# A two-layer trunk: new load and matmul orders in the first stage, fewer edge operations, deeper weight prefetch and a rearranged tail in the last output stage

## Chip, cores and metric

One core of one Trainium2 chip. The metric is the device time of one execution in microseconds (us), as a median of several runs. The engines are TensorE (PE), VectorE (DVE), ScalarE (ACT), GpSimd (POOL) and SyncE (SP), which here issues the transfers between HBM and on-chip memory (SBUF); TensorE's results land in PSUM banks.

## What is computed

One denoising step of a hybrid trunk with two layers, on 128 context tokens and 1024 latent tokens of width 1024 (inner width 2048). Latent tokens get a position embedding over a grid that is 64 wide. Cut to what matters:

```python
def _layer(x, cond, p, kind, h0):
    shift, scale, gate = _ada(cond, w_ada, b_ada)          # silu(cond) @ w_ada + b_ada
    h = _rmsnorm(x, norm_g) * (1.0 + scale) + shift
    u, z = jnp.split(h @ w_in, 2, axis=-1)
    if kind == 0:
        y = _fourier_mix(u, p["w_fmix"], p["b_fmix"])      # real 2-D FFT by group, then a matmul
    else:
        ...                                                # convolution, two RG-LRU scans
    out = (y * jax.nn.silu(z)) @ w_out
    return x + gate * out, state

def _fourier_mix(u, w_fmix, b_fmix):
    ug = u.astype(jnp.float32).reshape(B, S, N_FGROUPS, FG_DIM)
    f = jnp.real(jnp.fft.fft2(ug, axes=(1, 3), norm="ortho"))
    y = jnp.einsum("bsgi,gij->bsgj", f, w_fmix).reshape(B, S, D_INNER)
    return y + b_fmix
```

Layer 0 is of kind 0, layer 1 of kind 1. Behind layer 1 stands one more RMSNorm with the weight `final_g`.

## The kernel before, in words

Every matmul of size is done in three (`mm3`, L238 to L240): operands are split into a high half in a rounded format and the low rest (`split`, L227 and L228, or `split_ops`, L433 and L437: the high half is a cast on ACT, the low half a subtraction on DVE, for some on POOL), and TensorE multiplies high by high, low by high and high by low. Tile names end in `h` and `l` accordingly.

**First stage (0 to about 109 us).** The Fourier transform over tokens is done as matmuls with DFT tables, before the projection: nine tiles of 128 tokens (`x0` the context, `x1` to `x8` the latents) are loaded, get their position embedding, are normalised (`norm`, L468 to L494), and are added and subtracted in pairs (`halves`, `d` L502 and `x` L505). Meanwhile the mixer's weights `w_fmix` are folded with a small DFT (`fold`; `Ah`, `Al`, `Bh`, `Bl` are its results), and the conditioning rows are made from `w_adaN` (`ada_part`; row copy `hot`, L578; columns `adc`). Results are scaled by the conditioning into `Qo` (odd frequencies) and `Qr` (even ones and the context; `put`, L616 on ACT, L620 on DVE). The columns of frequency zero and of the Nyquist frequency are replaced at the end by values collected in `k0r` (L747 to L764, then L769 and L770 for each of the eight blocks `c` of `Qr`).

This stage is written as a `Plan`: each operation is added with a planned cost and its reads and writes, a list scheduler then fixes the order on each engine, and operations given with two costs may go to DVE or POOL. Three strings set what is not left to it: `DORD` is the order of SP's loads (`x` tiles, `w` weights of the mixer, `t` DFT tables, `s` and `h` conditioning weights, `p` positions, `c` the small DFT, `a` a table for x0, `q` a table for the context, `L` the first projection weights), `PORD` and `RORD` are the order of the blocks on TensorE (`f` fold, `j` tables and pair n, `t` and `u` token matmuls, `s` and `h` conditioning, `o` and `q` results, `F` the last token matmuls `psF`, `U` the first half of the projection).

The position embedding is loaded as one 80x512 table; for each 128-token tile of the grid, DVE marks a one-hot matrix (`mark`, L413), TensorE spreads the table by it (`spread`, L417), and ACT copies four of six results to SBUF (`keep`, L427). Adds of it to x are L468 and L471.

**Mixer (to about 256 us).** A loop over eight groups `g`: `uweights(g + 1)` loads two weight tiles `uL`, `uR` and forms their sum and difference (L856, L857) and splits them; `umat(g)` multiplies them with `Qo` and `Qr` (accumulators `pu`, splits `uh` L888 and `ul` L889); `ymat(g - 1)` applies the folded weights (`pa`, `p`, `qb`, `y`). At `g == 0` stands the `prologue` (L802): the Nyquist row `nyq`, and `rb`, the inverse norms of all tokens spread over the partitions (nine scalings `dg` of the identity, L828, matmuls L829, copies to SBUF). POOL streams the normalised input of the z projection through `norm_stream` (L839): load `nt`, add positions (L792), multiply by `rb` (L844), apply the conditioning (L846), store to `hD`; three of 24 pieces in each group. Behind the loop, `h_load` reads them back (`hr`, `hh`, `hl`), and the last `ymat` stands behind the first of these in program order.

**z stage, output stage of layer 0, layer 1, output stage of layer 1 (256 to 1483 us).** Outside the Plan, the framework's own scheduler orders the instructions; program order, dependencies and the number of buffers of each pool decide what may go early. `out_stage` (L1043) multiplies three column chunks `c` of 384 tokens with eight tiles `m` of `w_out`, each in two half tiles that are loaded two half tiles ahead; on each result DVE adds the residual (L1107), ACT squares it (L1113), DVE sums the squares into `ssum` (L1114). In layer 1, `norm_steps` turns the sum into an inverse norm: matmuls with ones (`r`, L1054), small operations, `dg` (L1059), a matmul that spreads it (`b`, L1067); then DVE multiplies the eight results by it and by `final_g` (L1455), and SP stores each to `yT`.

Of the kernel before, what the change touches and what calls it, by code (L numbers as in the profile page):

```python
# [32 lines left out]
PORD = 'j0 f0 t40 f1 j1 f2 u42 t41 f3 s0 u52 j2 s1 t62 j3 t63 s2 s3 o0 h0 u74 u64 o3 o6 o4 o7 h1 q0 o1 q1 o2 o5'  # L33
RORD = 'h2 F2 F0 F4 h3 F5 F3 F1 F7 U0 F6 U1'
# [153 lines left out]
def body(tc, nc, a):  # L188
# [147 lines left out]
    P = Plan({"raw": 3, "hi": 4, "lo": 4, "xs": 4, "d": 2, "dr": 2, "dh": 4, "ps": 8}, fixed=("SP", "PE"), handles={"DVE": V, "POOL": PL})  # L336
# [63 lines left out]


    hot = xp.tile([128, 512], F32, name="hot")
    posR, posC = [None] * 4, [None] * 2
    for n, (kind, i) in enumerate((("R", 0), ("C", 0), ("R", 2), ("C", 1), ("R", 1), ("R", 3))):
        oh = hot[:, i * 128:i * 128 + 128]
        lo, hi = (0, 64) if kind == "C" else (64, 80)

        def mark(kind=kind, i=i, oh=oh, lo=lo, hi=hi):
            if kind == "C":
                e = ident[lo:hi, 32 * i:32 * i + 32].rearrange("p (o c) -> p o c", o=1).broadcast_to([64, 4, 32])  # L410
            else:
                e = ident[lo:hi, 64 + 4 * i:68 + 4 * i].rearrange("p (r o) -> p r o", o=1).broadcast_to([16, 4, 32])
            V.tensor_copy(oh[lo:hi].rearrange("p (r c) -> p r c", r=4), e)  # L413

        def spread(n=n, kind=kind, i=i, oh=oh, lo=lo, hi=hi):
            T["ps", f"p{n}"] = ps(f"pos{kind}{i}")
            PE.matmul(T["ps", f"p{n}"], oh[lo:hi], T["dr", "pos"][lo:hi], start=True, stop=True)  # L417
        xa(P.add("DVE", 0.22, mark, w=[("hot", n)]))
        xa(P.add("PE", 1.9, spread, r=[("hot", n), ("dr", "pos")], w=[("ps", f"p{n}")]))
        if kind == "R" and i % 2 == 0:  # L420
            posR[i] = ("ps", f"p{n}")
        else:
            key = (posC if kind == "C" else posR)[i] = ("pos" + kind, i)
# [40 lines left out]
    def norm(t):  # L464
        x = X[t]
        if t > 0:
            def pos0():
                V.tensor_tensor(T[x][:, 0:512], T[x][:, 0:512], T[posR[(t - 1) // 2]], op=ALU.add)  # L468
# [88 lines left out]
    def ada_part(part, j):  # L557
# [12 lines left out]
        i = P.add("PE", 1.5, mms, r=names + [("silZ", 0)], w=[p])  # L570
        if not part:
            xa(i)
        if j == 3:
            row, pt = ("hot", "row") if not part else ("d", "row"), ("ps", f"adc{part}")

            def rows():
                T[row] = hot if not part else xb.tile([128, D], F32, tag="d", name="arow", bufs=2)[:, 0:512]
                A.copy(T[row], T[p])  # L578
# [18 lines left out]
            k = [P.add("ACT", 0.58, rows, r=[p] + [("hot", n) for n in range(6)], w=[row]),  # L597
# [120 lines left out]
    Qr = []  # L718
# [855 lines left out]
```

## Time and profile before

| | |
|---|---|
| runs of the kernel before | 1499.46, 1504.72, 1507.64 us; median 1504.72 |
| the profiled execution | 1498.54 us, its span 1496.8 us |
| busy in it | PE 1452.2 (97%), DVE 1073.2 (72%), ACT 740.5 (49%), POOL 157.5 (11%) |
| mean granted TensorE clock | 0.99 |

The span is what the trace covers; 1.7 us of the execution lie around it. PE's share is an average: it is near 100% in long stretches and lower at the beginning and at the end. A granted clock of 1.0 is 2.4 GHz, 0.5 is 1.2 GHz.

### The profile page before, as it was taken

What the parts mean: (1) busy time and instruction counts of PE and PEld (TensorE: products, weight loads), DVE (VectorE), ACT (ScalarE), POOL (GpSimd) and SP (SyncE); (2) the same over time, 40 slices, a digit from 0 to 9 for tenths busy, and PEclk for the clock granted to TensorE, in tenths of its full rate; (3) what the DMA queues carried; (4) which work ended last, traced back from release to release, by engine and by line L of the source; (5) the groups of instructions that cost most, each with busy time, mean ns of one, the idle gap of its engine ahead of it and who ended that gap; (6) DMA issues with size and microseconds to landing.
All of it is one profiled execution on the core that took longest, in us unless ns stands there. A gap on an engine that the chain in (4) does not pass through costs nothing. (4 is left out here: it accounts for less than half of the span.)

```text
span 1496.8 us, 21486 instructions
## 1 busy us (share of the span) xinstructions
PE 1452.2 (97%) x8370; PEld 1414.3 (94%) x8370; DVE 1073.2 (72%) x1596; ACT 740.5 (49%) x1113; POOL 157.5 (11%) x165
## 2 busy tenths in 40 slices
PE   7888999999999999999999999999999999999996
PEld 4578999999999999999999999999999999899996
DVE  7775455798864486747888787878788888686453
ACT  6552233322222354526866666666675758464331
POOL 2026785000001001000000000000000000000000
PEclk9998999999999999999999999999999999999998
DMA  6643657887665567531111111111111111786451
GB/s 222 200 130 117 178 188 266 302 269 247 223 212 162 184 195 240 187 126 43 59 59 60 57 59 58 59 59 58 59 59 59 59 58 65 231 287 206 148 189 48
DMA packets 83926, 212.73 MB, mean 142 GB/s; under 512 B 11424, under 2 KB 42656, under 8 KB 83696
## 3 DMA queue, kind: packets, MB, share of 16 engines
q1 hardware_dynamic: 83824, 211.36, 43.2%
q8 instruction: 65, 1.06, 0.3%
q14 instruction: 37, 0.30, 0.1%
HBM read 171.98 MB, written 39.35 MB: 141 GB/s over the span
## 5 line engine op out<-in xcount | busy, mean ns | idle before, releaser
L270 DVE SCALAR_TENSOR_TENSOR sil1j<-wada,sil 128x1024 bf16<-128x1024 f32 x64 | 78.1, 1220 | 9.9 <-DMA wada<-w_ada 9.8
L1289 DVE SCALAR_TENSOR_TENSOR uc<-u,tab,uc 128x1156 f32<-128x1156 f32 (+2 forms) x54 | 69.3, 1288 | 15.7 <-ACT u L1272 14.4
L1348 DVE SCALAR_TENSOR_TENSOR nu<-ga,nu 128x1156 f32<-128x1156 f32 x32 | 43.5, 1358 | 47.4 <-ACT tr L1343 47.3
L1107 DVE SCALAR_TENSOR_TENSOR x<-o,ada,xr 128x128 f32<-128x128 f32 (+1 forms) x64 | 31.6, 513 | 58.1 <-PE o L240 57.5
L1326 ACT ACTIVATE tr<-g,gb 128x386 f32<-128x386 f32 (+1 forms) x96 | 54.8, 584 | 22.0 <-PE g L240 21.0
L227 ACT CAST gh<-gr 128x384 fp32r<-128x384 f32 x80 | 39.7, 511 | 49.6 <-DMA gr<-gD 48.4
L1275 ACT ACTIVATE uc<-u,tab 128x386 f32<-128x386 f32 (+1 forms) x48 | 32.3, 673 | 61.4 <-PE u L240 61.4
L792 POOL TENSOR_TENSOR xr<-xr,tab 128x384 f32<-128x384 f32 (+1 forms) x24 | 23.0, 961 | 367.6 <-DMA xr<-xT 334.3
L228 DVE TENSOR_TENSOR gl<-gr,gh 128x384 fp32r<-128x384 f32 x80 | 42.1, 555 | 24.0 <-ACT gh L227 24.0
L1401 ACT ACTIVATE szz<-zz 128x386 f32<-128x386 f32 (+1 forms) x48 | 23.6, 495 | 71.9 <-PE zz L240 71.8
L1371 POOL COPY st<-nu 128x1 f32<-128x1 f32 x16 | 6.8, 426 | 495.5 <-DVE nu L1370 495.4
L888 ACT CAST uh<-pu 128x256 fp32r<-128x256 f32 (+1 forms) x32 | 12.7, 398 | 84.9 <-PE pu L240 84.8
L1326 ACT ACTIVATE ti<-g,gb 128x386 f32<-128x386 f32 (+1 forms) x96 | 51.6, 579 | 5.8 <-PE g L240 5.7
L889 DVE TENSOR_TENSOR ul<-pu,uh 128x256 fp32r<-128x256 f32 (+1 forms) x32 | 14.4, 454 | 49.7 <-ACT uh L888 49.6
L1358 DVE SCALAR_TENSOR_TENSOR ti<-ti,uc 128x1156 f32<-128x1156 f32 x32 | 43.5, 1358 | 7.6 <-ACT ti L1326 7.3
L1332 ACT ACTIVATE nu<-tr,sp2p 128x1156 f32<-128x1156 f32 x32 | 43.5, 1358 | 1.5 <-ACT tr L1326 0.4
L1354 DVE SCALAR_TENSOR_TENSOR tr<-ga,tr 128x1156 f32<-128x1156 f32 x32 | 43.5, 1361 | 0.7
L1362 DVE TENSOR_TENSOR ti<-ti,tr 128x1156 f32<-128x1156 f32 x32 | 43.4, 1357 | 0.4
L1336 ACT ACTIVATE ga<-tr,sm 128x1156 f32<-128x1156 f32 x32 | 43.2, 1349 | 0.1
L1373 DVE TENSOR_TENSOR_SCAN nu<-ga,tab,ti 128x1155 f32<-128x1155 f32 x16 | 41.9, 2619 | 0.1
L1370 DVE TENSOR_TENSOR_SCAN nu<-ga,ti 128x1156 f32<-128x1156 f32 x16 | 40.9, 2559 | 0.3
L227 ACT CAST gh<-sz 128x384 fp32r<-128x384 f32 x16 | 8.2, 514 | 63.1 <-DVE sz L1009 63.1
(1818 smaller groups left out, 5611.1 us busy)
## 6 DMA issues: line engine op xcount, KB each, us to landing
wo<-w_out SPq DMA_DIRECT2D x96, 512.0 KB, 4.2
wz<-w_z SPq DMA_DIRECT2D x32, 512.0 KB, 4.3
wada<-w_ada SPq DMA_DIRECT2D x32, 512.0 KB, 4.3
gr<-gD SPq DMA_DIRECT2D x80, 192.0 KB, 4.2
yD<-y SPq DMA_DIRECT2D x16, 576.0 KB, 4.8
zy<-yD SPq DMA_DIRECT2D x16, 576.0 KB, 6.9
wada<-w_adaN SPq DMA_DIRECT2D x16, 512.0 KB, 5.4
wu<-w_u SPq DMA_DIRECT2D x16, 512.0 KB, 3.6
```

Source lines behind the costliest of these rows:

```text
L227: A.copy(hi, src)
L228: (eng or V).tensor_tensor(lo, src, hi.bitcast(F32), op=ALU.subtract)
L270: V.scalar_tensor_tensor(junk, w, 0.5, sil[:, q, :], op0=ALU.mult, op1=ALU.mult, accum_out=ada[:, layer, mt, q:q + 1])
L1289: V.scalar_tensor_tensor(T["uc", m][:, lo:hi], T[ut][:, lo + t:hi + t], convw[:, m, t:t + 1], T["uc", m][:, lo:hi], op0=ALU.mult, op1=ALU.add)
L1326: A.activation(T[tg, n][:, lo:hi], T["ps", p][:, 0:hi - lo], AF.Tanh, scale=0.5, bias=gb2[:, 2 * d + mat, m:m + 1])
L1332: A.activation(T["nu", n], T["tr", n], AF.Tanh, scale=sp2[:, d, m:m + 1], bias=sp2[:, d, m:m + 1])
L1336: A.activation(T["ga", n], T["tr", n], AF.Exp, scale=sm4[:, d, m:m + 1], bias=sm4[:, d, m:m + 1])
L1348: V.scalar_tensor_tensor(T["nu", n], T["ga", n], 1.0, T["nu", n], op0=ALU.add, op1=ALU.mult)
L1354: V.scalar_tensor_tensor(T["tr", n], T["ga", n], 1.0, T["tr", n], op0=ALU.add, op1=ALU.mult)
L1358: V.scalar_tensor_tensor(T["ti", n], T["ti", n], 1.0, T["uc", m], op0=ALU.add, op1=ALU.mult)
L1362: V.tensor_tensor(ti, ti, T["tr", n], op=ALU.mult)
L1373: V.tensor_tensor_scan(nu[:, 0:L][:, ::-1], ga[:, 0:L][:, ::-1], ti[:, 0:L][:, ::-1], h0[:, 1, m:m + 1], ALU.mult, ALU.add)
```

## The change

In the first stage the position embedding is loaded ready for use: six tiles of 128x512 (`p0` to `p3` for rows, `p4` and `p5` for columns) in place of the table, the marks, the matmuls and the copies, and both adds of it may go to DVE or POOL. The three order strings are new, the planned cost of a conditioning block is 1.1 in place of 1.5, and `hot` is a tile of its own. `Qr` is one tile for its high and one for its low half over all eight `c`, so the sixteen operations on its edge columns become two. The `rb` part of the prologue is a function that is called behind `ymat(0)` at `g == 1`; `norm_stream` therefore does four pieces in each of the groups 1 to 6. The sums and differences for groups 1 and 2 are on DVE. In `out_stage` the weights are fetched three half tiles ahead; in layer 1's last chunk the last square is not added to `ssum` but summed by TensorE into the same accumulator, and the products of `m` 4 and 5 go to POOL, with `final_g` applied ahead by ACT and with a copy of `b` in SBUF.

```diff
+PM = (4, 5)
-DORD = 'p a x1 c x5 x6 x2 w0 t0 t1 x8 w1 x3 w3 x7 w2 s0 t2 t3 s1 x4 s2 s3 s4 s5 t4 s6 q s7 x0 h0 t5 h1 h2 h3 t6 h4 h5 h6 h7 L'
+DORD = 'p4 a x1 p2 p0 c x5 w0 x2 x6 p5 w1 t0 t1 p1 x3 x7 w2 t2 s0 w3 p3 s1 t3 x4 h0 h1 x8 s2 s3 s4 s5 s6 t4 s7 h2 q h3 t5 t6 x0 h4 h5 h6 h7 L'
...
+    def f_pos(n):
+        kw = dict(tag="pos", bufs=2) if n < 4 else {}
+        xa(fetch((posR + posC)[n], lambda: xp.tile([128, 512], F32, name=f"pos{n}", **kw), a["pos"][n], 256))
...
-        xa(P.add("DVE", 0.22, mark, w=[("hot", n)]))
-        xa(P.add("PE", 1.9, spread, r=[("hot", n), ("dr", "pos")], w=[("ps", f"p{n}")]))
...
-            xa(P.add("ACT", 0.58, keep, r=[("ps", f"p{n}")], w=[key]))
...
-            xa(P.add("DVE", 0.68, pos0, port=pk[0] != "ps", r=[pk], w=[x]))
+            xa(P.add("DVE", (0.68, 1.29), pos0, r=[posR[(t - 1) // 2]], w=[x]))
...
-    def zero(c):
-        kh = Qr[c][0][:, 0, 128:258:129]
-        V.tensor_copy(kh, k0r[:, c, :])
-        V.tensor_tensor(Qr[c][1][:, 0, 128:258:129], k0r[:, c, :], kh.bitcast(F32), op=ALU.subtract)
-    for c in range(KD):
-        P.add("DVE", 0.3, lambda c=c: zero(c), r=[("k0r", c)], w=[("Qr", c)])
+    def zero():
+        kh = Qrt[0][:, :, 0, 128:258:129]
+        V.tensor_copy(kh, k0r)
+        V.tensor_tensor(Qrt[1][:, :, 0, 128:258:129], k0r, kh.bitcast(F32), op=ALU.subtract)
+    P.add("DVE", 0.4, zero, r=ke, w=[("Qr", c) for c in range(KD)])
...
+        def rows():
 
             for c, (lo, hi) in enumerate(OC):
                 pr = ps2(f"rb{c}")
...
+            eng = V if g < 3 else PL
+            eng.tensor_tensor(e, L, Rr, op=ALU.add)
+            eng.tensor_tensor(L, L, Rr, op=ALU.subtract)
...
                 ymat(g - 1, prev)
-            for c, k in ns[3 * g:3 * g + 3]:
+            if g == 1:
+                rows()
+            for c, k in ns[4 * max(g - 1, 0):4 * g] if g < G - 1 else ():
                 norm_stream(c, k)
...
+                todo = [(t, i) for t in (ssum, *last) for i in range(3)]
+                for n, (t, i) in enumerate(todo):
+                    PE.matmul(pr[:, 2 * i:2 * i + 2], t[:, i * 128:i * 128 + 128], ones[:, 0:2],
+                              start=n == 0, stop=n == len(todo) - 1)
...
-            if n + 2 < len(steps):
-                c2, m2, hf2 = steps[n + 2]
+            for c2, m2, hf2 in steps[n + 2 if n == 0 else n + 3:n + 4]:
...
+                if (layer, c, m) == (1, 2, KD - 1):
+                    tail = (sq,)
+                else:
+                    tail = ()
+                    V.tensor_tensor(ssum, ssum, sq, op=ALU.add)
+            if (layer, c) == (1, 2) and m in PM:
+                A.activation(x, x, AF.Identity, scale=fing[:, m:m + 1])
...
+            if c == 2:
+                b = op.tile([128, 384], F32, tag="sq", name="b2", bufs=2)
+                A.copy(b, pb[:, 0:384])
+            for m in [m for m in range(KD) if c < 2 or m not in PM]:
                 V.scalar_tensor_tensor(xt[m], xt[m], fing[:, m:m + 1], pb[:, 0:384], op0=ALU.mult, op1=ALU.mult)
+                SY.dma_start(a["yT"][m][:, lo:hi], xt[m])
+            for m in PM if c == 2 else ():
+                PL.tensor_tensor(xt[m], xt[m], b, op=ALU.mult)
                 SY.dma_start(a["yT"][m][:, lo:hi], xt[m])
```

Three places of the order show how instructions move; a row is a line of the kernel, its operation and its tiles, and the lines of the changed kernel have other numbers.

DVE at the end of the first stage, before: the zeroing operations (`Qrh<-k0r`, `Qrl<-k0r`) behind the `dg` scalings, two blocks at a time between wide passes.

```order
L747 COPY k0r<-psF_1015 128x2
L828 TENSOR_SCALAR dg_1210<-tab,rs 128x128 x3
L761 TENSOR_TENSOR k0r<-k0r,coef 128x16
L762 TENSOR_SCALAR kb<-coef 128x8
L763 TENSOR_SCALAR kb<-coef 128x8
L889 TENSOR_TENSOR ul_0_1146<-pu_0_0_980,uh_0_1145 128x256
L828 TENSOR_SCALAR dg_1220<-tab,rs 128x128 x3
L828 TENSOR_SCALAR dg_1230<-tab,rs 128x128 x3
L764 TENSOR_TENSOR k0r<-k0r,kb 128x16
L620 SCALAR_TENSOR_TENSOR Qrl_827<-psF_1015,coef,Qrh_826 128x2x129
L769 CAST Qrh_814<-k0r 128x2
L770 TENSOR_TENSOR Qrl_815<-k0r,Qrh_814 128x2
```

The same place in the changed kernel, behind the difference `uL` for group 1:

```order
L740 TENSOR_TENSOR k0r<-k0r,coef 128x16
L741 TENSOR_SCALAR kb<-coef 128x8
L742 TENSOR_SCALAR kb<-coef 128x8
L229 TENSOR_TENSOR e1l<-e_1040,e1h 128x1024
L869 TENSOR_TENSOR ul_1_1108<-pu_1_0_996,uh_1_1107 128x256
L743 TENSOR_TENSOR k0r<-k0r,kb 128x16
L598 SCALAR_TENSOR_TENSOR Qrl<-psF_939,coef,Qrh 128x2x65
L598 SCALAR_TENSOR_TENSOR Qrl<-psF_930,coef,Qrh 128x2x65
L229 TENSOR_TENSOR o1l<-uL_1036,o1h 128x1024
L787 MEMSET zt 128x1024
L748 CAST Qrh<-k0r 128x8x2
L749 TENSOR_TENSOR Qrl<-k0r,Qrh 128x8x2
```

The scalings stand earlier, the sums for group 1 have come in, and both zeroing operations (L748, L749) stand together behind `o1l` and the memset `zt`. `Qol` and `Qoh` parts of `pu` don't need them, each matmul with `Qrh` or `Qrl` now does.

ACT around the row copy `hot`, before: it stands behind the square of x0 (`x_644`) and the two steps on its norm.

```order
L480 ACTIVATE jk_668,nc_209<-x_644 128x1024
L483 ACTIVATE nc_209<-nc_209,eps 128x1
L484 ACTIVATE nc_209<-nc_209,epsh 128x1
L578 COPY hot<-ada_560 128x512
L494 ACTIVATE x_644<-x_644,rs 128x1024
```

In the changed kernel (x0 is `x_701`):

```order
L429 CAST dh_621<-dr_594 128x512
L556 COPY hot<-ada_466 128x512
L594 ACTIVATE Qoh_170<-psO_347,coef 128x512
L594 ACTIVATE Qoh_172<-psO_357,coef 128x512
L594 ACTIVATE Qoh_174<-psO_365,coef 128x512
L594 ACTIVATE Qoh_176<-psO_373,coef 128x512
L594 ACTIVATE Qoh_178<-psO_560,coef 128x512
L594 ACTIVATE Qoh_180<-psO_546,coef 128x512
L412 CAST d_0h<-d_0_606 128x1024
L412 CAST d_1h<-d_1_628 128x1024
L412 CAST s_0h<-x_222 128x1024
L458 ACTIVATE jk_740,nc_208<-x_701 128x1024
```

The copy stands ahead of six scalings `Qoh`, three casts and the square of x0 (`jk_740`).

SP's first loads, before: x5 (`x_238`), x6 and x2 are the sixth to eighth.

```order
L242 DMA tab<-tab 128x760
L348 DMA drpos<-pos 80x512
L348 DMA dralt<-alt 128x272
L348 DMA x_229<-x_all 128x1024
L348 DMA drfc<-fdft 128x512
L348 DMA x_238<-x_all 128x1024
L348 DMA x_241<-x_all 128x1024
L348 DMA x_250<-x_all 128x1024
L348 DMA wf_259<-w_fmix 128x1024
```

In the changed kernel x5 is the eighth (`x_231`), x2 and x6 the tenth and eleventh, and the last column tile of the positions the twelfth.

```order
L243 DMA tab<-tab 128x760
L349 DMA pos_213<-pos 128x512
L349 DMA dralt<-alt 128x272
L349 DMA x_222<-x_all 128x1024
L349 DMA pos_224<-pos 128x512
L349 DMA pos_226<-pos 128x512
L349 DMA drfc<-fdft 128x512
L349 DMA x_231<-x_all 128x1024
L349 DMA wf_233<-w_fmix 128x1024
L349 DMA x_239<-x_all 128x1024
L349 DMA x_246<-x_all 128x1024
L349 DMA pos_254<-pos 128x512
```

In both output stages the rows of all engines are the same in both kernels, but for the tail of layer 1.

## Rows read from the trace of the kernel before

**Rows 1.** Windows: stretch, length, busy per engine, mean granted clock, DMA share, GB/s
```profile
104.00:130.00 26.00, 19.26 (x108) 17.96 (x107) 19.61 (x47) 5.29 (x9) 9.68 (x4) 0.74 0.26 84
130.00:256.00 126.00, 123.08 (x908) 121.75 (x907) 62.71 (x162) 41.34 (x92) 98.10 (x94) 1.00 0.62 196
...
660.00:1277.00 617.00, 614.70 (x3479) 612.97 (x3478) 498.90 (x526) 410.03 (x550) 11.79 (x31) 1.00 0.18 59
```

**Rows 2.** Waits of TensorE, 16 to 130 us: total, times, longest (us)
```profile
PE pu L239 <- DVE Qrl L770: 4.0, 2, 3.7
PE fold L238 <- ACT wf0h L433: 3.9, 1, 3.9
PE adc L583 <- ACT hot L578: 2.4, 1, 2.4
PE psO L238 <- DVE Bl L540: 2.1, 1, 2.1
PE pu L238 <- DVE Qrh L769: 1.9, 1, 1.9
...
PE pu L240 <- DVE e0l L437: 1.1, 1, 1.1
PE pu L239 <- DVE Qrl L620: 0.8, 1, 0.8
```

**Rows 3.** Windows, the stretch behind the waits for Qr
```profile
122.00:126.00 4.00, 4.00 (x19) 4.00 (x20) 0.76 (x7) 0.00 (x0) 0.00 (x0) 0.50 0.46 137
```

**Rows 4.** Timeline of DVE, 100 to 122 us: start, length, operation
```profile
100.29 1.27 DVE L620 SCALAR_TENSOR_TENSOR Qrl<-psF,coef,Qrh 128x258 fp32r<-128x258 f32 x4
...
105.54 5.52 DVE L828 TENSOR_SCALAR dg<-tab,rs 128x128 f32<-128x128 f32 x6
...
114.05 0.91 DVE L809 MEMSET zt<- 128x1024 f32 x1 [0.15 <-DVE Qrh L769]
...
114.95 1.22 DVE L228 TENSOR_TENSOR o1l<-uL,o1h 128x1024 fp32r<-128x1024 f32 x1
...
119.44 2.29 DVE L770 TENSOR_TENSOR Qrl<-k0r,Qrh 128x2 fp32r<-128x2 f32 x1
```

**Rows 5.** Timeline of POOL, 104 to 124 us
```profile
108.34 2.44 POOL L857 TENSOR_TENSOR uL<-uL,uR 128x1024 f32<-128x1024 f32 x1
...
119.34 2.38 POOL L857 TENSOR_TENSOR uL<-uL,uR 128x1024 f32<-128x1024 f32 x1
```

**Rows 6.** Timeline of ACT, 60 to 70 us
```profile
67.09 1.06 ACT L480 ACTIVATE jk<-x 128x1024 bf16<-128x1024 f32 x1 [6.15 <-DMA x<-x_all]
```

**Rows 7.** Windows of the first 20 us, and the timeline of DVE there
```profile
0.00:10.00 10.00, 5.38 (x6) 1.49 (x6) 3.58 (x17) 2.65 (x4) 0.20 (x4) 1.00 0.62 197
10.00:20.00 10.00, 6.40 (x7) 1.66 (x6) 8.73 (x18) 9.23 (x16) 0.00 (x0) 1.00 0.73 267
...
16.85 1.28 DVE L502 SCALAR_TENSOR_TENSOR d<-x,rs,x 128x1024 f32<-128x1024 f32 x1
```

**Rows 8.** Timelines of DVE and SP behind the last matmul of the output
```profile
1484.50 0.56 DVE L1114 TENSOR_TENSOR ssum<-ssum,sq 128x384 f32<-128x384 f32 x1 [0.65 <-ACT sq L1113]
...
1488.97 4.29 DVE L1455 SCALAR_TENSOR_TENSOR x<-x,tab,b 128x384 f32<-128x384 f32 x8 [1.15 <-PE b L1067]
...
1489.62 4.19 SPq L1456 DMA_DIRECT2D yT<-x  x8
```

**Rows 9.** Timelines of POOL and TensorE at both ends of the mixer
```profile
133.36 1.49 POOL L792 TENSOR_TENSOR nt<-nt,tab 128x256 f32<-128x256 f32 x2 [0.65 <-DMA nt<-xT]
...
247.70 4.24 POOL L228 TENSOR_TENSOR hl<-hr,hh 128x384 fp32r<-128x384 f32 x4
...
254.60 0.42 PE L238 MATMUL qb<-uh,Bh 128*128 128x322 f32 x1 [2.88 <-ACT p L906]
```

**Rows 10.** Timeline of TensorE, last output stage
```profile
1310.97 0.44 PE L238 MATMUL o<-gh,wo1040h 128*128 128x384 f32 x1 [1.41 <-ACT wo1040h L227]
```

**Rows 11.** Groups by line and shape on POOL: count, busy, mean ns
```profile
L792 POOL TENSOR_TENSOR nt<-nt,tab 128x384 f32<-128x384 f32 x16 | 15.0, 940 | 20.4 <-DMA nt<-xT 20.4
```

More of the change, by code (lines that the diff above doesn't have):

```diff
@@ L334, in ps @@
         return pp.tile([128, 512], F32, tag="ps", name=name)
-    P = Plan({"raw": 3, "hi": 4, "lo": 4, "xs": 4, "d": 2, "dr": 2, "dh": 4, "ps": 8}, fixed=("SP", "PE"), handles={"DVE": V, "POOL": PL})
+    P = Plan({"raw": 3, "hi": 4, "lo": 4, "xs": 4, "d": 2, "dr": 2, "pos": 2, "dh": 4, "ps": 8}, fixed=("SP", "PE"), handles={"DVE": V, "POOL": PL})
     T, xa_ops = {}, []
@@ L576, in rows @@
             def rows():
-                T[row] = hot if not part else xb.tile([128, D], F32, tag="d", name="arow", bufs=2)[:, 0:512]
+                T[row] = xb.tile([128, 512], F32, name="hot") if not part else xb.tile([128, D], F32, tag="d", name="arow", bufs=2)[:, 0:512]
                 A.copy(T[row], T[p])
@@ L596, in cols @@
                         V.scalar_tensor_tensor(o, o, 1.0, rowed(normg[:, 0, ms]), op0=ALU.add, op1=ALU.mult)
-            k = [P.add("ACT", 0.58, rows, r=[p] + [("hot", n) for n in range(6)], w=[row]),
+            k = [P.add("ACT", 0.58, rows, r=[p], w=[row]),
                  P.add("PE", 1.0, turn, r=[row, ("silZ", 0)], w=[pt])]
@@ L724, in switch @@
         p = hqb_cm.__enter__()
-        Qr.extend([[p.tile([128, 2, NF - 256], F32R, name=f"Qr{i}{c}") for i in "hl"] for c in range(KD)])
+        Qrt.extend(p.tile([128, KD, 2, NF - 256], F32R, name=f"Qr{i}") for i in "hl")
+        Qr.extend([[t[:, c] for t in Qrt] for c in range(KD)])
     sw = P.add("X", 0.0, switch, after=xa_ops, lat=0.0)
@@ L1048, in out_stage, with norm_steps @@
             gt[0, k] = gt0.get(k) if layer == 0 else g_load(layer, 0, k)
-        def norm_steps(c, ssum, xt):
+        def norm_steps(c, ssum, xt, last=()):
             def sums():
                 pr = ps(f"r{layer}{c}")
-                for i in range(3):
-                    PE.matmul(pr[:, 2 * i:2 * i + 2], ssum[:, i * 128:i * 128 + 128], ones[:, 0:2], start=True, stop=True)
+                todo = [(t, i) for t in (ssum, *last) for i in range(3)]
+                for n, (t, i) in enumerate(todo):
+                    PE.matmul(pr[:, 2 * i:2 * i + 2], t[:, i * 128:i * 128 + 128], ones[:, 0:2],
+                              start=n == 0, stop=n == len(todo) - 1)
                 r3 = op.tile([128, 3], F32, tag="r3", name=f"r3{layer}{c}", bufs=2)
@@ L1501, in constants @@
     posc = np.concatenate([np.sin(ac), np.cos(ac)], 1)
-    out = dict(tdft=tdft, pdft=pdft, fdft=fdft, alt=alt, pos=np.concatenate([posc, posr], 0),
+    out = dict(tdft=tdft, pdft=pdft, fdft=fdft, alt=alt, pos=np.stack([np.repeat(posr[4 * i:4 * i + 4], 32, 0) for i in range(4)] + [np.tile(posc[32 * i:32 * i + 32], (4, 1)) for i in range(2)], 0),
                posRT=posr.T.reshape(4, 128, 16).transpose(1, 0, 2), posCT=posc.T.reshape(4, 128, 64).transpose(1, 0, 2),
```

43 lines of the change are left out of this document (9 added, 34 removed).

## The prediction

> **What bounds the kernel now.** I first read the busy time of each engine by stage [rows 1]. From 660 to 1277 us TensorE is busy for 614.70 of 617 us: the recurrent layer is bound by its matmuls, and the change touches nothing there. The mixer from 130 to 256 us is nearly as full, 123.08 of 126. The part that is not full is the beginning: between 104 and 130 us TensorE works for 19.26 of 26 us, with a mean granted clock of 0.74. So the time that an edit can give back lies in front of 130 us, in one wait near 254 us, in the waits of the last output stage, and behind the last matmul.
>
> Next I read what TensorE waited for between 16 and 130 us [rows 2]. The list is short: the first fold of the mixer's weights (3.9 us), the low half `Bl` of a fold (2.1), the row copy `hot` (2.4), the low half of the first even weight (1.1), and three waits for the edge columns of `Qr`, which belong together: 4.0, 1.9 and 0.8 us. Stalls also cost clock: between 122 and 126 us, behind the `Qr` waits, TensorE is busy throughout at a granted clock of 0.50, which is 1.2 of 2.4 GHz [rows 3].
>
> Then I asked what VectorE (DVE) and GpSimd (POOL) did during the `Qr` waits [rows 4, 5]. DVE needs 5.52 us for six small scalings (L828) while POOL adds and subtracts 128x1024 tiles (the second from 108.34 on, 2.44 us); it needs 2.29 us for a two-column subtraction (L770) at 119.44, which ends just after POOL's 2.38 us operation at 119.34. The tiny zeroing operations are not slow by themselves. They stand in order behind wide passes, and those stand behind POOL.
>
> **The change, part by part.** Sums go against the profiled execution's 1498.54 us. Its three unprofiled companions have a median of 1504.72, 6.2 us more, so I forecast a difference and put it on the median.
>
> *The `Qr` edge and what stands around it.* Three edits meet here: sixteen two-column operations become two over all eight columns; the nine `dg` scalings and the `rb` copies leave the prologue; and the even/odd sums of the next two weights go from POOL to DVE. The four sums that POOL no longer does took about 2.4 us each; on DVE a pass of that shape takes 1.22 [rows 4], so DVE gains 4.9 us of work in this stretch, and loses the waiting for POOL, which cost more: the six scalings alone stretch over 5.52 us. But the two new operations need the whole of `k0r` and write the whole of `Qr`, and the order of the changed kernel puts them behind `ul_1`, two `Qrl` writes, `o1l` and the memset. TensorE reaches its first `Qrh` matmul before they are done. The wait that remains: 1.22 for `o1l`, 0.91 for the memset, and about seven small operations (cast `uh`, `ul`, one `k0r`, two `Qrl`, the two zeroings) at the 0.32 us that four `Qrl` writes average (1.27 for four), 2.2 together: an estimate of 4.3 us in one piece. Before it was 4.0 + 1.9 + 0.8 = 6.7. **Gain 2.4**, between 0 (DVE is also late with the added sums) and 6.7 (all of it hidden).
>
> *The clock there.* A mean of 0.74 over 26 us, with levels of 1.0 and 0.5, is 13.5 us at half clock; 4.8 of them were spent in two of the waits (4.0 and 0.8), so about 8.7 us of matmuls ran at half speed and lost 4.4 us. In the changed order one wait of about 4 us is followed by a dense run of matmuls, where before a second wait of nearly 4 us came late and kept the clock low behind it. The row shows 4 us of unbroken matmuls that are still at the low clock. [...] **I take 2.0 of the 4.4**, bounds 0 and 4.4.
>
> *New orders for loads and matmuls.* `hot` waited because ScalarE (ACT) took the square of x0 ahead of it, and ACT sat 6.15 us waiting for x0's load [rows 6]. In the changed order the copy stands before that square and before anything of x0: its 2.4 us go. What is late next is the cast `dh`, whose load comes early. The first even/odd sum moves from POOL (2.4) to DVE (1.22); that is 1.2 on the chain that TensorE waited 1.1 for. `Bl` stays behind a DVE pass, and POOL still does the split of `d_2`, so I allow 0.5 of its 2.1. **Together 4.0**, bounds 0 (each wait turns up at another block) and 5.6 (all three).
>
> *The start.* Six one-hot marks, six matmuls and four copies go; 1.4 MB more of loads come. Before, the first fold waited for the cast of its weights, in line behind the cast of `d_0`, whose difference DVE began at 16.85 [rows 7]. In the changed order the same cast stands behind the same `d_0`, but DVE passes the position add of x6 first, which needs everything up to the twelfth load of SP's list: 4.46 MB by the shapes in the list, where the first eight, 3.05 MB, sufficed. At 267 GB/s, the mean of 10 to 20 us [rows 7], the added 1.4 MB are 5 us; DVE and ACT in exchange have less to do, and the queue no longer waits for a buffer at 6 us. **I take 0**, between +4 (later) and −2.
>
> *`rb` moved behind the first `ymat`.* The three matmuls stay the same; they now use accumulator banks between two busy users. Two DVE reads of a bank at about 0.54 us (4.29 for eight, [rows 8]) can stand in front. **A loss of 0.5**, bounds 0 and 1.1.
>
> *The norm stream on POOL.* It can start only when `rb` exists, so about one block of the mixer later, 126/8 = 16 us, but two pairs of sums (9.6 us) are gone by then, and nothing runs in the first of the eight blocks. In 130 to 256 us POOL worked for 98.10 us [rows 1]; less the 4.24 us of `hl` at the end and less two pairs it has about 84 to do behind that start. The stream began at 133.36; with a start 16 us later it is through at about 235 if its loads keep up, a dozen us before the 247.70 at which the `hl` splits began [rows 9]. These held their buffers, and behind that came the 2.88 us wait of `qb` at 254.60. **Gain 1.5**, bounds 0 and 2.9.
>
> *Weights three half tiles ahead.* The order of loads, casts and matmuls in both output stages is word for word what it was; only `yT` at the very end differs. The scheduler had already lifted the loads as far as the buffers allow. So the two waits of 1.4 us each in the last output stage, for the two halves of the same weights (one shown in [rows 10]), stay. **0.**
>
> *The tail.* The sum on DVE, 0.56 us [rows 8], goes: TensorE adds the last square itself, straight behind ACT. The six `r` matmuls become three early and three late, the same shape. **0.65** with the gap beside it. The two products on POOL take 0.94 each [rows 11]. They need a copy of `b` to SBUF first (0.54 by the nearest rows, DVE's products), and SP issues the outputs in order, with POOL's first product second: 0.54 + 0.94 = 1.5 us behind `b` (at 1488.97), then seven issues at 0.52 (4.19 for eight) are 1494.1, where 1489.62 + 4.19 = 1493.8 stood before [rows 8]. **0**, bounds −0.7 and 1.
>
> Sum: 2.4 + 2.0 + 4.0 + 0 − 0.5 + 1.5 + 0 + 0.65 + 0 = **10.1 us faster** (rounded up from 10.05): 1488.4 for an execution like the profiled one, 1494.6 on the median, of which I give 1494.5.
>
> **Rivals.**
> *The waits only move (0.27).* TensorE waits for some other operand wherever a listed one is removed: a chain of DVE and ACT passes bounds the stage, not the places. For it: between 104 and 130 DVE is busy for 19.61 us, as long as TensorE. Against: parts of that are blocked passes, not work. Then only `Qr` (2.4), half the `qb` wait and the tail remain, less 0.5: about 4 faster, 1501.
>
> *The clock never falls (0.17).* Where all first-stage waits shrink together, the rest of the lost clock (2.4), 1.6 of `Bl` and 1.4 of `qb` come too: 15.5 us faster, 1489. For it: the low stretch begins behind the idle one. Against: the one-piece `Qr` wait.
>
> *The deeper weights do act (0.05).* The 2.8 us of the two waits in [rows 10] go in addition: 1491.7. Against: identical order.
>
> *The loads at the start decide the other way (0.05).* If x5, x6 and their position tiles come late, everything behind the first fold shifts by as much. With 4.46 MB at the mean rate of the first 10 us, 197 GB/s [rows 7], they land at 22.6 us, some 6 later than DVE began `d_0` before; for a result slower than before the shift must exceed the 10.1 us gained, so that they land at 27 us, at 165 GB/s. The Trainium skill ("SBUF — State Buffer", "SBUF: two separate sides") adds that a GpSimd operation locks DVE out for its whole length; four position adds are now on POOL among DVE's first passes, where two were, and by that rule the folds behind the first would be later again by as long as these run. The trace bears the rule out at L828, and no row shows it for this place. Slower by over 0.5% would be 1512.
>
> **How the numbers follow.** 0.5% (7.5 us) is about what a measurement of this kernel tells from no change; its own three runs span 8. My case has a chance of 0.46. Faster by over 0.5% (below 1497.2) come most of it (it is 2.7 us beyond the limit), the clock's rival and the weights': 0.64. Within 0.5%: the moving waits, the rest of my case, a mild start loss: 0.31. Slower: 0.05. The range goes from 1482 (the clock's rival, the start's 2 us, the weights' 2.8, and half of the 4.3 that stay of `Qr`'s wait) to 1504 (moved waits, and 3 of the start's 4 us).
>
> **What would show it.** Right: TensorE's wait for L748/L749 of the changed kernel is one piece of 3 to 5 us; no wait for `hot`; DVE's small operations near 105 us last under 0.5 us; `qb` waits less than 2 us; the stretch behind 1277 us still shows two waits of about 1.4 us; the span from the last `x` (L1107) to the last product is about 0.7 us shorter. Wrong: the first fold begins after 23 us; new waits of `fold`, `psO` or `ada` add up to more than 4 us; POOL's `nt` work ends after 248 us; `pu` waits over 2 us behind `rb`.

## The result, and the profile after

The changed kernel takes 1510.8 us (median of 11 runs) where the kernel before takes 1504.72 (median of 11): a ratio of 1.0052 with a 95% interval of 1.0037 to 1.0066. It is slower, by half a per cent, where the prediction had 10 us faster, and it lies above the range. The profiled executions stand the same way: 1508.89 us (span 1507.1) against 1498.54 (span 1496.8).

What TensorE waited for behind its first fold and up to 140 us, in the changed kernel (total, times, longest, in us; compare [rows 2]):

```profile
PE pu L239 <- DVE Qrh L748: 7.1, 1, 7.1
PE fold L240 <- DVE wf0l L416: 2.3, 1, 2.3
...
PE adc L561 <- ACT hot L556: 0.7, 1, 0.7
```

The list is shorter than before. `hot` waits 0.7 us instead of 2.4, the wait for `Bl` is gone, and the waits for the edge of `Qr` have become one piece, as foreseen, but of 7.1 us. The first stage as a whole is well ahead: the last group of `pu` is cast (`uh`) at 233.17 us, where it was at 243.00. Up to there the change gains 9.8 us. The cast in the kernel before:

```profile
243.00 1.68 ACT L888 CAST uh<-pu 128x256 fp32r<-128x256 f32 x4 [12.48 <-PE pu L240]
```

Then it loses more than that. The same view from 140 to 300 us:

```profile
PE qb L239 <- ACT p L886: 12.4, 2, 10.8
PE pa L239 <- ACT p L886: 6.1, 1, 6.1
```

Before there was one wait of 2.9 us here [rows 9]; now there are three, 18.5 us in all. They are waits for `p`, which ACT writes. The shortest, 1.6 us at 204.32, lies inside the mixer, ahead of the cast at 233.17, and is already in the 9.8: ACT stood 3.10 us for the difference `uL` of group 7, which POOL made late, behind a wait of 10.94 us for a load `nt` of the norm stream. The other two, 6.1 and 10.8 us, end the mixer at 244.17 and 260.85 us. ACT's own timeline shows what holds it there (a bracket is the idle time before an operation and what ended it):

```profile
233.17 1.66 ACT L868 CAST uh<-pu 128x256 fp32r<-128x256 f32 x4 [12.46 <-PE pu L241]
...
242.82 0.92 ACT L228 CAST hh<-hr 128x384 fp32r<-128x384 f32 x2 [6.35 <-DMA hr<-hD]
...
259.50 0.92 ACT L228 CAST hh<-hr 128x384 fp32r<-128x384 f32 x2 [14.18 <-DMA hr<-hD]
```

ACT stands for 6.35 and for 14.18 us at casts `hh` of the z stage's inputs, whose loads `hr` have not landed, and `p` is in line behind them. Those inputs come from the norm stream on POOL:

```profile
143.54 1.02 POOL L823 TENSOR_TENSOR nt<-nt,rb 128x384 f32<-128x384 f32 x1
...
252.63 0.99 POOL L823 TENSOR_TENSOR nt<-nt,rb 128x384 f32<-128x384 f32 x1
...
254.35 3.84 POOL L229 TENSOR_TENSOR hl<-hr,hh 128x384 fp32r<-128x384 f32 x4
```

In the kernel before:

```profile
137.73 3.95 POOL L844 TENSOR_TENSOR nt<-nt,rb 128x384 f32<-128x384 f32 x3
...
245.57 1.02 POOL L844 TENSOR_TENSOR nt<-nt,rb 128x384 f32<-128x384 f32 x1
```

The first multiplication by `rb` is at 143.54 us, where it was at 137.73, and the last ends at 253.6, where it ended at 246.6. The `hl` splits behind it begin at 254.35 instead of 247.70 [rows 9]. So TensorE arrives 9.8 us earlier at a place whose inputs arrive 6.7 us later. The remaining loss comes with the two stalls themselves, in the clock (stretch, length, busy per engine, granted clock, DMA share, GB/s):

```profile
246.00:248.00 2.00, 2.00 (x10) 2.00 (x10) 1.95 (x9) 0.00 (x0) 1.54 (x2) 0.50 0.77 245
...
260.00:262.00 2.00, 1.15 (x4) 1.15 (x5) 1.37 (x3) 2.00 (x7) 0.00 (x0) 0.50 0.75 256
...
264.00:266.00 2.00, 2.00 (x8) 2.00 (x8) 1.84 (x8) 0.00 (x0) 0.00 (x0) 0.50 1.01 388
266.00:268.00 2.00, 2.00 (x12) 2.00 (x11) 2.00 (x8) 1.58 (x4) 0.00 (x0) 0.90 0.81 314
```

TensorE resumes at 244.17 us and runs at the low clock (1.2 GHz) to about 249.3; behind the second stall it resumes at 260.85 us (254.60 before) and runs at the low clock for some 6 us. That costs about half of the 5.2 and of the 5.6 us that it is busy there. In the kernel before the clock stayed at 1.0 through this place. The second column chunk of z is done 8.6 us later than before (ACT takes it at 280.25 instead of 271.68), and the last residual add comes at 1493.20 instead of 1483.23: the rest is 1.4 us of short waits in the two output stages (for `gh` 2.9 us in five waits where it was 0.5, for the weights `wo1040` 2.0 where it was 2.8). The tail adds 0.35.

### The profile page after: what moved, and what is told of

Same layout as the page of the kernel before. It is cut to its first block, busy times and chain, and to the rows that moved or that the text cites. A ratio compares the mean times of both kernels' runs of the same rounds, so it can differ in the third digit from the quotient of the medians.

```text
span 1507.1 us, 21445 instructions
## 1 busy us (share of the span) xinstructions
PE 1437.4 (95%) x8364; PEld 1412.2 (94%) x8364; DVE 1067.1 (71%) x1576; ACT 740.6 (49%) x1112; POOL 151.8 (10%) x164
## 3 DMA queue, kind: packets, MB, share of 16 engines
q8 instruction: 65, 1.06, 0.3%
## 5 line engine op out<-in xcount | busy, mean ns | idle before, releaser
L868 ACT CAST uh<-pu 128x256 fp32r<-128x256 f32 (+1 forms) x32 | 12.6, 397 | 86.3 <-PE pu L241 86.1
L989 ACT ACTIVATE sz<-z 128x384 f32<-128x384 f32 x48 | 23.1, 488 | 48.8 <-PE z L241 28.8
```

## The experiments

**Theory A:** the norm stream takes about 110 us from its first multiplication to its last, wherever it starts, because each of its 24 pieces must be loaded, worked on and stored through three buffers and one in-order queue; moving `rb` started it too late, and the z stage waits for its end. **Theory B:** what is late is only the split `hl`, which POOL does behind the whole stream and which holds the raw buffers that the next loads need. **Theory C:** the loss sits in the output stages and the tail.

**1. `rb` back in the prologue, three pieces in each group again** (all else as changed):

```diff
                 prologue()
+                rows()
...
-            if g == 1:
-                rows()
-            for c, k in ns[4 * max(g - 1, 0):4 * g] if g < G - 1 else ():
+            for c, k in ns[3 * g:3 * g + 3]:
```

> The changed kernel with rb made in the prologue again (group 0) and three pieces of the norm stream in each group, all else as changed. Theory A (the stream starts too late, because rb moved): the first nt multiplication by rb comes about 10 us earlier than at 143.5 us, the stream ends near 245 instead of 255 us, TensorE's waits for p shrink from 18.5 to about 8 us, and the kernel is 9 to 11 us faster than the changed one, about 1500 us. Theory B (the hl splits on POOL hold the raw buffers until the stream is over): the same here, since the splits move with the stream's end. Theory C (the loss sits in the output stages and the tail): no change within 2 us.

Measured: 1497.46 us, 0.9957 of the kernel before (0.9937 to 0.9976), some 13 us below the changed kernel. TensorE's waits behind 140 us, and three rows of POOL:

```profile
PE pa L239 <- ACT p L886: 3.1, 1, 3.1
PE qb L239 <- ACT p L886: 2.1, 1, 2.1
```

```profile
129.58 3.97 POOL L823 TENSOR_TENSOR nt<-nt,rb 128x384 f32<-128x384 f32 x3
...
180.34 3.29 POOL L770 TENSOR_TENSOR nt<-nt,tab 128x384 f32<-128x384 f32 x3 [10.77 <-DMA nt<-xT]
...
240.15 0.99 POOL L823 TENSOR_TENSOR nt<-nt,rb 128x384 f32<-128x384 f32 x1
```

The stream runs from 129.58 to 241.1 us, 111.5 us; in the changed kernel it ran from 143.54 to 253.6, 110.1; before, from 137.73 to 246.6, 108.9. Its start moved by 14 us between the two changed versions and its length by one. That is what theory A expects, and the gain is a little above it. The run does not show what sets the length.

**2. The first `hl` splits on DVE** (the changed kernel otherwise):

```diff
-                split(r[:, j, :], h, lw, PL if c == 0 and k + j < 4 else V)
+                split(r[:, j, :], h, lw, V)
```

> The changed kernel with the first four hl splits of the z inputs on DVE instead of POOL, stream and rb untouched. Theory B: the raw buffers come free as soon as DVE has split them, the loads of the next inputs go out about 10 us earlier, the waits of 6.1 and 10.8 us for p go, TensorE runs the last ymat and the first two column chunks of z while the stream ends, and at most some 4 us of wait appear at the third chunk: 11 to 15 us faster than the changed kernel, about 1497 us. Theory A: the z stage needs the end of the stream anyway, so the wait moves into z and the gain is under 5 us. Theory C: no change.

Measured: 1512.62 us, 1.0058 (1.0036 to 1.0079): no gain over the changed kernel. The waits stay, and ACT still finds the loads late:

```profile
PE qb L239 <- ACT p L886: 15.4, 2, 12.9
PE pa L239 <- ACT p L886: 5.5, 1, 5.5
```

```profile
256.95 0.92 ACT L228 CAST hh<-hr 128x384 fp32r<-128x384 f32 x2 [13.19 <-DMA hr<-hD]
```

Theory B is out: DVE has split the first four inputs by 237.5 us, and still all but three of the loads `hr` go out only from 253.73 us on, straight behind the stream's last stores (251.65). Freeing the raw buffers earlier does not help while SP's order has these loads behind the stream.

**3. The new first stage alone** (ready positions, order strings, one `Qr` tile; `rb`, stream, sums on POOL, output stages and tail as before):

```diff
-            eng = V if g < 3 else PL
+            eng = PL
...
+            for c, k in ns[3 * g:3 * g + 3]:
...
-PM = (4, 5)
+PM = ()
...
+            if n + 2 < len(steps):
+                c2, m2, hf2 = steps[n + 2]
```

> The kernel before with only the new first stage (loads of ready positions, three order strings, one Qr tile); rb, the norm stream, the sums on POOL, the output stages and the tail as before. Theories A and B: the first stage gains about 8 to 10 us up to the mixer, the stream starts earlier by nearly as much, and the kernel is 6 to 10 us faster than before, about 1497 us, with at most 5 us of waits for p. Theory C agrees in the sign. Against all of them: no faster than before, if the gain of the first stage depends on the sums on DVE and on dg being out of the way.

Measured: 1497.55 us, 0.9951 (0.9936 to 0.9967). The first stage is the part of the change that gains, 7 us, and it does so with the sums on POOL too. Experiment 1 has the sums on DVE, the deeper weight prefetch and the new tail besides, and takes the same time: together these three are worth nothing that can be measured.

**4. The tail as before** (the changed kernel with `PM = ()` and the last square added by DVE):

```diff
-                if (layer, c, m) == (1, 2, KD - 1):
+                if False:
...
-            if c == 2:
+            if False:
```

> The changed kernel with the tail of before: last square added by DVE, all eight products on DVE. The profile of the changed kernel shows the path from the last residual add to the end 0.35 us longer than before, so all theories expect 0.3 to 0.4 us less here, no difference that can be measured. Theory C would want at least 3 us.

Measured: 1511.36 us, 1.0047 (1.0033 to 1.0062), against 1.0052 for the changed kernel: no difference. Experiments 1 and 3, one with the new output stages and one with those of before, agree as well, so theory C is out.

**5. The kernel before with nothing but `rb` moved:**

```diff
+            if g == 1:
+                rows()
-            for c, k in ns[3 * g:3 * g + 3]:
+            for c, k in ns[4 * max(g - 1, 0):4 * g] if g < G - 1 else ():
```

> The kernel before with one part of the change alone: rb made behind the first ymat in group 1, four pieces of the norm stream in each of the groups 1 to 6. Theory A (the stream takes about 110 us whatever its start, and the z stage waits for its end): the first multiplication by rb comes 10 to 15 us later than at 137.7 us, the stream ends near 260 instead of 247.7 us, the wait of qb grows from 2.9 to 10 us or more, and the kernel is 9 to 14 us slower than before, about 1515 us. Rival (the new first stage is needed for the loss, because it brings TensorE early to the end of the mixer): under 4 us slower.

Measured: 1519.96 us, 1.0121 (1.0102 to 1.0141), 17 us slower than the kernel before, more than expected. TensorE's waits, and the first and last multiplication by `rb`:

```profile
PE qb L238 <- ACT p L907: 10.0, 1, 10.0
PE pa L238 <- ACT p L907: 5.9, 1, 5.9
```

```profile
154.62 1.01 POOL L845 TENSOR_TENSOR nt<-nt,rb 128x384 f32<-128x384 f32 x1
...
263.00 0.99 POOL L845 TENSOR_TENSOR nt<-nt,rb 128x384 f32<-128x384 f32 x1
```

The stream starts at 154.62 and ends at 264.0, 109.4 us. The rival fell: the move alone costs more than the whole change, and the new first stage hides a part of it by bringing the mixer forward (the stream starts 11 us earlier in the changed kernel).

**6. Four pieces in each of the groups 0 to 5, with `rb` in the prologue** (against experiment 1):

```diff
-            for c, k in ns[3 * g:3 * g + 3]:
+            for c, k in ns[4 * g:4 * g + 4]:
```

> As the kernel with rb in the prologue (1497.46 us), but with four pieces of the norm stream in each of the groups 0 to 5 instead of three in each of eight. If the groups of the mixer set the stream's pace, it ends 10 us or more earlier than at 242 us, TensorE's waits for p (5.2 us there) go, and the time is about 1492 us. If the three buffers and the order of SP's queue set the pace, the stream still takes some 110 us and the time stays within 2 us.

Measured: 1495.59 us, 0.9958 (0.9943 to 0.9973), like experiment 1. The stream takes 111 us again (127.31 to 238.6). So the groups of the mixer don't set its pace.

**7. The two `silD` stores in group 0 instead of group 2.** They write the conditioning vector to HBM in 4-byte pieces, 4 KB each. In experiment 1 SP issues them at 167.60 us, and the three loads `nt` behind them:

```profile
167.60 1.20 SPq L925 DMA_DIRECT2D silD<-silT  x2
168.90 6.56 SPq L821 DMA_DIRECT2D nt<-xT  x3
```

POOL then waits 10.77 us for the first of these loads (the second row of POOL above); the slowest of the three took 11.3 us to land, where 2.6 is the median of all. In the kernel before, the wait behind the stores was 5.74 us, so it is not 11 us in all profiles. The edit, against experiment 1, sends the stores behind the weights of group 1:

```diff
             nxt = uweights(g + 1) if g + 1 < G else None
+            if g == 0:
+                for q in range(2):
+                    tc.keep_in_program_order(SY.dma_start(silD[0, q].rearrange("(k p) -> p k", p=128), silT[:, :, q]))
             uv = umat(g, uw)
...
-            if g == 2:
-                for q in range(2):
-                    tc.keep_in_program_order(SY.dma_start(silD[0, q].rearrange("(k p) -> p k", p=128), silT[:, :, q]))
```

> As the kernel with rb in the prologue, but with the two stores of silT in 4-byte pieces (silD) sent in group 0 instead of group 2. In all profiles POOL waits about 11 us in one piece for the nt loads behind these stores. If the stores are what holds the queue, that wait shrinks to under 3 us, the stream ends 5 to 9 us earlier, TensorE's waits for p go, and the time is 4 to 6 us less, about 1492 us. If the wait is that of the nt buffers themselves, nothing changes within 2 us.

Measured: 1490.34 us, 0.992 (0.9906 to 0.9935), 7 us below experiment 1 (by the ratios, 5.6). The stream, and TensorE's wait for `Qr`:

```profile
130.18 3.94 POOL L823 TENSOR_TENSOR nt<-nt,rb 128x384 f32<-128x384 f32 x3
...
233.06 1.02 POOL L823 TENSOR_TENSOR nt<-nt,rb 128x384 f32<-128x384 f32 x1
```

```profile
PE pu L239 <- DVE Qrh L748: 10.8, 1, 10.8
```

The stream is 103.9 us long, the waits for `p` are gone. At the new place the load of `uR` for group 1, issued just ahead of the stores, lands after 9.0 us instead of 4.8, and the wait for `Qr` grows from 7.2 to 10.8 us: part of the gain is given back.

**8. The two operations on `Qr`'s edge on POOL** (with `rb` in the prologue; against experiment 1):

```diff
-        V.tensor_copy(kh, k0r)
-        V.tensor_tensor(Qrt[1][:, :, 0, 128:258:129], k0r, kh.bitcast(F32), op=ALU.subtract)
+        PL.tensor_copy(kh, k0r)
+        PL.tensor_tensor(Qrt[1][:, :, 0, 128:258:129], k0r, kh.bitcast(F32), op=ALU.subtract)
-    P.add("DVE", 0.4, zero, r=ke, w=[("Qr", c) for c in range(KD)])
+    P.add("POOL", 0.4, zero, r=ke, w=[("Qr", c) for c in range(KD)])
```

> As the kernel with rb in the prologue, but with the two operations on the edge columns of Qr on POOL, which is idle there, instead of DVE, where they stand behind o1l (1.21 us) and the memset (0.91 us). If these two are part of the 7.1 us that TensorE waits in one piece, the wait shrinks by about 2 us to some 5 us, and the time is 1 to 3 us less, about 1495.5 us. If it is set by something else ahead, nothing changes.

Measured: 1494.54 us, 0.995 (0.9933 to 0.9967); its interval overlaps that of experiment 1. The wait:

```profile
PE pu L239 <- POOL Qrh L748: 6.2, 1, 6.2
```

One us shorter, not two: POOL's cast takes 1.00 us beside DVE's `o1l`, where it took 0.11 on DVE. `o1l` and the memset, 2.1 us, are not the main part of a wait of 7; what stands ahead of them is.

**9. The `silD` stores in the first stage's plan,** behind x0's load, and no longer in the loop (against experiment 1):

```diff
+        elif kind == "z":
+            def f_sil():
+                for q in range(2):
+                    SY.dma_start(silD[0, q].rearrange("(k p) -> p k", p=128), silT[:, :, q])
+            P.add("SP", 0.9, f_sil, w=[("silD", 0)], lat=2.0)
...
-x0 h4 h5 h6 h7 L'
+x0 z h4 h5 h6 h7 L'
```

> As the kernel with rb in the prologue, with the two silD stores given to the first stage's plan, behind x0's load at about 68 us, where SP waits for buffers, instead of behind the weights of group 1, where they delayed the load of uR by some 6 us and TensorE's wait for Qr rose from 7.2 to 10.8 us. Expected: that wait is 7 us again, the stream is as short as with the stores in group 0 (104 us), no waits for p: 3 to 4 us below 1490.3, about 1487 us. If the stores disturb something here too, it stays near 1490 us.

Measured: 1498.67 us, 0.9974 (0.9957 to 0.9992): a miss. TensorE's waits up to 140 us:

```profile
PE ada L551 <- DMA wada<-w_adaN: 6.0, 1, 6.0
PE pu L239 <- DVE Qrh L753: 5.6, 1, 5.6
```

There are no waits for `p`, but TensorE now waits 6.0 us for a load of conditioning weights behind the stores (between 70 and 90 us these loads land after 12.3 us in the median, 4.7 in the kernel before), and the first `pu` matmul comes at 99.86 us, 8.4 later than in experiment 7. What is behind the stores is late here too.

**10. Experiment 9 with the `Qr` edge on POOL and the two last products on DVE.**

> The same with the two operations on the edge columns on POOL (measured alone about 3 us) and with the two last products on DVE again (the last square still summed by TensorE). Expected: TensorE's wait for Qr 5 to 6 us, the path from the last residual add to the end 0.6 us shorter than before, no waits for p, about 1484 to 1485 us.

Measured: 1497.12 us, 0.996 (0.9942 to 0.9978): a miss, with the same sign: 4.9 us of wait for the conditioning weights, and the first `pu` matmul at 99.01 us.

**11. The kernel before with the `silD` stores in its plan,** by the edit of experiment 9.

> The kernel before with the silD stores alone moved to the first stage's plan. Its stream ends at 247.7 us and TensorE waits 2.9 us for p, so that the stream is only a little late: the stream ends 6 us or more earlier, the 2.9 us go, and the time is 2 to 3 us less, about 1500.5 us. If the stores were not in the way here (its 5.7 us wait is not theirs), no change.

Measured: 1503.17 us, 1.0011 (0.9995 to 1.0026): no change. Its stream ended 3 us earlier and the 2.9 us of `qb` went, but 5.3 us of waits for conditioning weights came.

**12. The stores behind the weights of group 2** (group 1 in the loop), the `Qr` edge on POOL, all eight products on DVE, the last square summed by TensorE (against experiment 7; the lines for POOL are those of experiment 8):

```diff
-            if g == 0:
+            if g == 1:
...
-PM = (4, 5)
+PM = ()
```

> As the kernel of 1490.3 us (rb in the prologue, silD early), but with the two silD stores behind the weights of group 2 (about 103 us, where the next load is wanted 10 us later), the two operations on Qr's edge columns on POOL, and the two last products on DVE. If the stores hold up whatever load is in flight for about 9 us and nothing is wanted in that time here, TensorE's wait for Qr is 5 to 6 us instead of 10.8, there are no waits for p and no longer waits for weights, and with 0.6 us from the tail the time is 5 to 7 us below 1490.3, about 1484 us. If the stores delay the weights of group 2 so that pu waits, it stays at 1488 us or more.

Measured: 1490.39 us, 0.9909 (0.9887 to 0.9931), the runs between 1483.5 and 1492.53. The profiled execution, of 1484.61 us, looks as expected:

```profile
PE pu L239 <- POOL Qrh L748: 6.0, 1, 6.0
```

```profile
126.67 3.94 POOL L823 TENSOR_TENSOR nt<-nt,rb 128x384 f32<-128x384 f32 x3
...
229.90 1.01 POOL L823 TENSOR_TENSOR nt<-nt,rb 128x384 f32<-128x384 f32 x1
```

The wait for `Qr` is 6.0 us, none for `p` is left, and the stream is over at 230.9 us, as the last `uh` casts begin (230.86). The load `uL` that SP issues 3 us behind the stores lands after 12.6 us (4.2 is the median of these loads), but nothing waits for it. Its ratio is the lowest here, 0.9% below the kernel before and 1.4% below the changed one, but neither by the ratio nor by the median is it told apart from experiment 7.

## Why the prediction was wrong, step by step

**The step that failed is the norm stream on POOL.** I counted POOL's work (about 84 us), set it behind a start 16 us later, and concluded that it is through at about 235 us "if its loads keep up". They don't, and did not before. What POOL waited for between the first and the last multiplication, in the kernel before and in the changed one:

```profile
POOL nt L792 <- DMA nt<-xT: 21.7, 13, 5.7
```

```profile
POOL nt L770 <- DMA nt<-xT: 28.1, 11, 10.9
```

The work was sized about right: 81.1 us in the changed kernel, 86.1 in the one before. But with 5 us less to do the stream is no shorter, because POOL waits 6.4 us more for its loads: it takes 109 us in the kernel before and 109 to 112 in every version with the `silD` stores in group 2, with pieces three or four to a group. The `if` carried the whole term, and [rows 9] had the number that decides it: 133.36 to 247.70 is 114 us, in which POOL worked for 91.5. So a gain of 1.5 us became 16.9 us of waits at the mixer's end, 1.6 ahead of it and two spells of low clock. Experiments 1 and 5 show from both sides that the start sets the end, and 2, 4 and 6 exclude the splits, the tail and the groups.

What sets the length is shown in part. The `silD` stores are 4 to 8 us of it: with the stores elsewhere the stream takes 104 to 105 us (experiments 7 and 9 to 12). For the rest the waits point to the loop of three buffers: in the changed kernel SP's loads `nt` stood 16.0 us, in eleven waits, for a store `hD` to land. No run changed the number of buffers or gave the stream a queue of its own, so that part stays open.

**The mixer's front gained 9.8 us where my terms gave 7.9.** Their split was wrong. The load and matmul orders gave more: the first `pu` matmul comes at 90.86 instead of 98.83 us, 8.0 us for the 4.0 that I gave the orders and the start together (the first fold begins at 19.51 instead of 20.31). TensorE from the first fold to the first `pu` matmul, before and after (stretch, length, busy, granted clock, DMA share, GB/s):

```profile
20.31:98.83 78.52, 70.80 (x360) 0.96 0.53 181
```

```profile
19.51:90.86 71.35, 65.83 (x368) 1.00 0.56 190
```

Beside the 0.8 us of the start, idle time fell by 2.2 us (7.7 to 5.5) and busy time by 5.0. Most of the latter is clock, which the terms counted only behind 104 us: before, TensorE ran at the low clock near 52 to 55 and 93 to 96 us, behind the waits for `Bl` and for the conditioning weights and rows, and in the changed kernel it does not. At 0.96 over 78.5 us that is an estimated 3.1 us; what the other 1.9 are stays open. `Qr` gave less: the one-piece wait is 7.1, not 4.3, where the separate waits were 6.7, so the gain of 2.4 became a loss of 0.4. DVE's timeline there:

```profile
92.84 2.24 DVE L807 TENSOR_SCALAR dg<-tab,rs 128x128 f32<-128x128 f32 x3
...
95.39 1.25 DVE L807 TENSOR_SCALAR dg<-tab,rs 128x128 f32<-128x128 f32 x6
...
97.61 1.21 DVE L836 TENSOR_TENSOR e<-uL,uR 128x1024 f32<-128x1024 f32 x1
...
99.15 1.21 DVE L837 TENSOR_TENSOR uL<-uL,uR 128x1024 f32<-128x1024 f32 x1
...
100.51 1.21 DVE L229 TENSOR_TENSOR e1l<-e,e1h 128x1024 fp32r<-128x1024 f32 x1
...
102.59 1.21 DVE L229 TENSOR_TENSOR o1l<-uL,o1h 128x1024 fp32r<-128x1024 f32 x1
103.96 0.91 DVE L787 MEMSET zt<- 128x1024 f32 x1 [0.16 <-DVE o1l L229]
104.79 0.11 DVE L748 CAST Qrh<-k0r 128x16 fp32r<-128x16 f32 x1
```

TensorE runs out of work at 98.0 us. The passes `e`, `uL` and `e1l`, 1.21 us each, which I had counted as done by then, only start at 97.61: the sums that moved to DVE are themselves in the path. Experiment 8 agrees: going around the last two passes gave 1 us. The first two rows show DVE held up beside POOL once more: three `dg` scalings take 2.24 us beside POOL's `o0l` (92.20 to 94.60), and six take 1.25 after it. The Trainium skill ("SBUF — State Buffer", "SBUF: two separate sides") gives GpSimd and VectorE a shared port that one of them holds for a whole instruction; these rows agree.

**The clock** behind `Qr` was right: low from about 103 to 109 us, over 4.4 us of matmuls, a loss of 2.2 where it was 4.4; I had taken 2.0 of gain. The clock was missed elsewhere: in front of 100 us, where it gained, and behind the two stalls at the mixer's end, where it lost some 5 us.

**`rb` itself** made no wait for TensorE (0.5 was expected, within its bounds of 0 to 1.1). **The weights** changed little, as the order said: the waits for the two halves of `wo1040` are 1.2 and 0.8 us, for 1.4 and 1.4.

**The tail** was right for the square and wrong for the copy. From the start of the last residual add to the end of the last `dg` it takes 3.93 us instead of 4.59, 0.66 for the 0.65 forecast. Then ACT's copy of `b` comes between, and DVE's products wait for it too:

```profile
1498.93 0.48 ACT L1445 COPY b<-b 128x384 f32<-128x384 f32 x1 [3.38 <-PE b L1051]
```

```profile
1496.45 0.68 DVE L1043 TENSOR_SCALAR dg<-tab,r 128x128 f32<-128x128 f32 x3
1499.44 3.24 DVE L1447 SCALAR_TENSOR_TENSOR x<-x,tab,b 128x384 f32<-128x384 f32 x6 [2.31 <-ACT b L1445]
```

The products begin 6.24 us behind the residual add, 5.74 before, and the last store is issued 10.94 us behind it, 10.58 before. Part of that is the clock: the spreading matmul `b` took 1.65 us at a granted clock of 0.50, where it took 1.06 before, at 1.00 as it began. Without these 0.59 us the path is 10.35, 0.23 shorter than before. In experiment 12, which has no copy and the same 1.65, it is 10.51, so the copy took back 0.43 of the 0.66. By its median experiment 4 can't tell the two tails apart; in its profile, where the clock fell earlier still, the old tail took 11.52.

**The rivals.** None was this one. The slower case that I gave a chance was the start's loads; the start did nearly as I took it, 0.8 us earlier. The lock that this rival feared for the folds behind the first did show, but small: `wf0l` took 2.29 us beside POOL's position adds, 1.22 before, and the second fold waited 2.3 us for it instead of 1.3. The observation that I had listed, "POOL's `nt` work ends after 248 us", came true.

What stays open: why the medians of experiments 7 and 12 agree while the profiled executions differ by 6.6 us (1491.23 and 1484.61), and why the waits for `gh` in the output stages grew.

## What to carry to other kernels

A producer that streams through a few buffers has a length of its own: read it as last end minus first start, not as the sum of its operations, and treat a later start as a later end, unless a run shows that it has slack. When a stage is brought forward, look at what it will meet there: work that was just in time before is late after. And when an order table already hides something (here `rb` early in the prologue), ask what hangs on the end of the chain that it starts, before moving it for a wait at its beginning.

## What was not expected of the hardware

Two stores of 4 KB each, in 4-byte pieces, took 10.5 to 13.3 us to land wherever they stood (11.8 in the kernel before, 10.9 to 11.2 in experiment 7, 12.2 to 13.3 in experiment 9, 10.5 to 10.8 in experiment 11), and transfers near them in the queue were late too: a load `nt` of 192 KB landed after 11.3 us instead of 2.6, the load of `uR` just ahead of the stores in experiment 7 after 9.0 us instead of 4.8, and the load of `uL` behind them in experiment 12 after 12.6 us instead of 4.2. An engine waited for a load beside them (`nt` 10.8 us, `uR` with 3.6 us more for `Qr`, conditioning weights 6.0 us) everywhere but in experiment 12. The Trainium skill ("DMA: Bandwidth & Descriptors", "Why small descriptors are slow (HBM only)") gives each transfer piece a fixed overhead; these runs agree in the direction, and show besides that loads around them land late.
